# Decoder layer on one core: 22 instead of 20 of 24 gate tiles in pairs of seven products, with the products' banks, the t4 product and the next block's roots moved

## The chip, the cores and the metric

The kernel runs on one core of a Trainium2 chip. Its engines are PE (TensorE: matmuls, and PEld, the weight loads of the same engine), DVE (VectorE), ACT (ScalarE), POOL (GpSimd) and SP (SyncE, which issues nearly all DMAs here). The metric is the device time of one execution, in microseconds (us); lower is better.

## The reference

One layer of a hybrid decoder, for 2048 prompt tokens and 8 sequences of 8 sample tokens, in float32. With `xn = rmsnorm(x)`, one projection of 1024 inputs gives the columns of three branches and of 24 gate tiles; the branches (attention over a window of 128, a short convolution, a gated MLP with 128x128 position mixing) are merged through sigmoid gates:

```
r = rsqrt(mean(x*x) + EPS);  xn = x * r * norm_w
h = xn @ w_in                                   # q k v z_a | B C h z_b | u v_c z_c | g (3*1024 columns)
y_a, y_b, y_c = attention, conv, spatial MLP
a, b, c = (silu(z_i) * y_i) @ w_out_i           # 512 -> 1024 each
m = sigmoid(g_a)*a + sigmoid(g_b)*b + sigmoid(g_c)*c
y = x + m @ w_o
```

## The kernel before

**Blocks.** The tokens are worked in four blocks (`SBS`), one after the other: three of 512 tokens, and a last one of 512 prompt and 64 sample tokens (n = 576, in chunks of 288). Activations stand as channels x tokens, in tiles of 128 channels. Every float32 operand is split into a high and a low part (`split`: a cast on ACT, `wh` or `xh`, then a subtraction on DVE, `wl` or `xl`), and every product is three matmuls (L231 to L233: wh*xh, wh*xl, wl*xh).

**Weights.** `order()` lists the units of weights. `take` gives the next one and has the two behind it split (L222 on ACT, L223 on DVE) into one of four `wh`/`wl` buffers, and some more loaded (L140 on SP) into one of three `raw` buffers.

**Gate phase.** In each block 24 gate tiles (three for each of eight output tiles) are multiplied (8 k-tiles each) and put through a sigmoid, and `merge` multiplies each by its branch's output product (4 k-tiles, L231 to L233 again, then L897 and L903 on DVE). The first `SINGLES` = 4 tiles are done singly (`single`), the other 20 in ten pairs (`pair`). A pair treats two tiles, two halves of k and two halves of the tokens as a 2x2 block product in seven products of 4 k-tiles at half the tokens (`product`, L929 to L931) instead of eight. Four of the seven use sums of blocks: sums of weights, made on POOL (`halves`: s1 at L154, a difference in place at L155, s2 at L160, s2 again at L164), and sums of activations t1 to t4, made on DVE from `xh + xl` (`x_sums`: L840, L848 to L852 for t1 to t3 in `first`; L840 and L864 for t4 in `last`). Each t is split like any operand. The results are added up on DVE (L949 to L959), two sigmoids follow, and two merges.

**PSUM banks.** The seven products are put, in their order, on S0, pv, S1, S0, S1, pv, S0. A bank is free for the next product when the addition that reads it is done. Merges and single tiles use the three banks of `ps_mm`, transposes and the spatial products the two of `ps_tp`.

**Next block's roots.** `xrstd` gives pieces for the next block's `rsqrt`: four pieces (five ahead of the last block) that load 128 tokens into a `raw` buffer (L260 on SP) and sum their squares (L261 on ACT), then `fin` (L218 and L219 on POOL: scale and power) and `spread` (L275: transposes on PE that spread the roots over the partitions, and a copy on ACT).

**Order.** PE and SP run in the order in which the code is written; `later(delay, piece)` puts a piece behind so many ticks of written matmul work (a single tile is 1.5 ticks, a pair 2.75), and `flush` puts all pending ones at once. What DVE, ACT and POOL do is ordered by a scheduler when the kernel is built, and each engine then works its list strictly in that order. At the start of the gate phase there are still pieces pending from the MLP: the spatial products (L783, L784 on PE, two for each 128 tokens), their sums (L786, L787, L762 on DVE, in a tile `sp`) and the split into `br2`. The tiles `sp`, `s1` and `s2` share two buffers (tag `side`); t4 takes the buffer that the MLP's `suc` leaves when the last L762 has read it.

## Time and profile before

| | |
|---|---|
| runs | 2015.57 us median of 3 (2015.36 to 2016.91) |
| the profiled execution | 2013.36 us, its span 2011.6 us |
| PE | 1972.3 us busy, 98% of the span, 11771 matmuls |
| DVE, ACT, POOL | 68%, 47%, 17% busy |
| chain of work that ended last | PE 89%, DVE 5%, ACT 4% |
| gate phase until the first pair, block 0 | 253.88 to 290.98 us of the span |
| the same, block 2 | 1201.47 to 1249.57 us |

Start times are microseconds from the start of the span. A row of the timeline has the start, the duration, the engine, line and operation, out<-in, sizes, and in brackets how long the engine had been idle ahead of it and what released it. Matmuls overlap, so that the distance between two starts is their price, not the duration that stands in a row. In the table by windows the columns are the stretch, its length, the busy time and number of instructions of PE, PEld, DVE, ACT and POOL, the granted clock of TensorE (1.00 is full speed), the DMA share and GB/s. In the table of waits they are the waiting engine and line, what was waited for, and the total, the number and the longest in us.

### The profile page before, as it was taken

Reading aid. Unit: us, or ns where it says so; the run is one execution under the profiler, and the core shown is the slowest. Engines: PE = TensorE matmul, PEld = TensorE weight load, DVE = VectorE, ACT = ScalarE, POOL = GpSimd, SP = SyncE. Lnnn points to the kernel's source line nnn. Section 1 sums busy time; section 2 is a strip of 40 time slices with the busy share of each in tenths; the row PEclk is TensorE's granted clock in tenths of the full one; section 3 lists DMA queues with packets and bytes.
Section 4 is the critical chain, followed back from the end, with each engine's and each line's share of the span. In section 5 each row is a group of like instructions: output and inputs, shape, how many; then the busy total and the mean of one; then the engine's idle time right before and its main releaser. Section 6 shows DMA issues by size and latency. Waiting matters only on the chain.

```text
span 2011.6 us, 30272 instructions
## 1 busy us (share of the span) xinstructions
PE 1972.3 (98%) x11771; PEld 1765.4 (88%) x11771; DVE 1365.2 (68%) x2367; ACT 945.1 (47%) x1679; POOL 335.0 (17%) x294
## 2 busy tenths in 40 slices
PE   6999999999999999999999998999999999999999
PEld 5888889998888889998888887999889999999999
DVE  5688377875588558777478736777647873587772
ACT  4775254442576344444367524444347743333340
POOL 2100024320100004440200002442020000133310
PEclk9999999999999999999999998999999999999999
DMA  6222233336222232226322223223622242222233
GB/s 209 90 79 84 84 126 115 102 115 224 95 73 74 94 114 101 101 95 207 129 84 74 87 76 123 97 95 115 229 87 56 62 114 69 71 82 87 95 101 109
DMA packets 85711, 212.44 MB, mean 106 GB/s; under 512 B 18224, under 2 KB 23344, under 8 KB 85552
## 3 DMA queue, kind: packets, MB, share of 16 engines
q1 hardware_dynamic: 85536, 209.53, 32.4%
q8 instruction: 92, 1.51, 0.3%
q10 hardware_dynamic: 32, 0.98, 0.1%
q14 instruction: 51, 0.42, 0.1%
HBM read 201.46 MB, written 10.00 MB: 105 GB/s over the span
## 4 chain that ended last, share of the span: by engine, by line
PE 89%; DVE 5%; ACT 4%; DMA 1%; issue 1%; POOL 1%; SPq 0%; ACTq 0%; DVEq 0%; POOLq 0%
PE ps_mm L231 18%; PE ps_mm L232 18%; PE ps_mm L233 18%; PE pairS L929 4%; PE pairS L930 4%; PE pairS L931 4%; DVE wl L223 3%; PE pairpv L930 2%; PE pairpv L929 2%; PE pairpv L931 2%; PE ps_mm L353 2%; PE ps_mm L352 2%; PE ps_mm L351 2%; ACT wh L222 2%; PE wideS L353 1%; PE wideS L352 1%
## 5 line engine op out<-in xcount | busy, mean ns | idle before, releaser
L223 DVE TENSOR_TENSOR wl<-raw,wh 128x1024 fp32r<-128x1024 f32 (+1 forms) x416 | 461.7, 1118 | 272.1 <-ACT wh L222 269.1
L222 ACT CAST wh<-raw 128x1024 fp32r<-128x1024 f32 (+1 forms) x416 | 354.7, 866 | 539.1 <-PE ps_mm L232 232.7
L231 PE MATMUL ps_mm<-xh,wh 128*128 128x512 f32 (+1 forms) x1280 | 460.2, 360 | 0.0
L233 PE MATMUL ps_mm<-xh,wl 128*128 128x512 f32 (+1 forms) x1280 | 451.7, 353 | 0.0
L232 PE MATMUL ps_mm<-xl,wh 128*128 128x512 f32 (+1 forms) x1280 | 451.6, 353 | 0.0
L233 PEld LDWEIGHTS ps_mm<-xh,wl 128*128 128x128 f32 x1280 | 241.0, 188 | 30.7
L232 PEld LDWEIGHTS ps_mm<-xl,wh 128*128 128x128 f32 x1280 | 241.5, 189 | 27.1
L231 PEld LDWEIGHTS ps_mm<-xh,wh 128*128 128x128 f32 x1280 | 241.3, 189 | 27.3
L222 ACT CAST wh<-s 128x512 fp32r<-128x512 f32 x120 | 70.9, 621 | 194.1 <-PE ps_mm L232 116.5
L929 PE MATMUL pairS<-xh,wh 128*128 128x256 f32 (+1 forms) x480 | 140.1, 292 | 8.1 <-DVE ca L949 7.9
L218 POOL TENSOR_SCALAR vr<-vssq 128x1 f32<-128x1 f32 (+1 forms) x17 | 5.4, 316 | 804.9 <-ACT vn L795 804.5
L931 PE MATMUL pairS<-xh,wl 128*128 128x256 f32 (+1 forms) x480 | 137.2, 286 | 0.0
L930 PE MATMUL pairS<-xl,wh 128*128 128x256 f32 (+1 forms) x480 | 137.1, 286 | 0.0
L231 PE MATMUL ps_mm<-mhi,wh 128*128 128x512 f32 (+1 forms) x320 | 112.5, 352 | 0.9 <-ACT mhi L222 0.9
L233 PE MATMUL ps_mm<-mhi,wl 128*128 128x512 f32 (+1 forms) x320 | 112.5, 352 | 0.0
L897 DVE TENSOR_TENSOR t<-ps_mm,t 128x512 f32<-128x512 f32 (+1 forms) x120 | 70.8, 593 | 58.5 <-PE ps_mm L233 57.3
L929 PEld LDWEIGHTS pairS<-xh,wh 128*128 128x128 f32 x480 | 91.2, 190 | 14.5 <-DVE ca L949 13.2
L154 POOL TENSOR_TENSOR s<-raw 128x512 f32<-128x512 f32 x40 | 56.8, 1419 | 243.1 <-DMA raw<-in_wt 192.2
L164 POOL TENSOR_TENSOR s<-raw,s 128x512 f32<-128x512 f32 x40 | 67.6, 1690 | 160.2 <-DVE wl L223 160.2
L930 PEld LDWEIGHTS pairS<-xl,wh 128*128 128x128 f32 x480 | 91.4, 190 | 1.2
L929 PE MATMUL pairS<-xsum,wh 128*128 128x256 f32 (+1 forms) x320 | 91.7, 287 | 0.0
L930 PE MATMUL pairS<-xsum,wh 128*128 128x256 f32 (+1 forms) x320 | 91.6, 286 | 0.0
(280 smaller groups left out, 4638.7 us busy)
## 6 DMA issues: line engine op xcount, KB each, us to landing
raw<-in_wt SPq DMA_DIRECT2D x208, 512.0 KB
raw<-in_wout SPq DMA_DIRECT2D x96, 256.0 KB
raw<-in_wn SPq DMA_DIRECT2D x40, 512.0 KB
raw<-in_wo SPq DMA_DIRECT2D x32, 512.0 KB
xraw<-in_xn SPq DMA_DIRECT2D x12, 512.0 KB
xt<-in_xt SPq DMA_DIRECT2D x24, 256.0 KB
out_yt<-xt SPq DMA_DIRECT2D x24, 256.0 KB
xbuf<-in_xt SPq DMA_DIRECT2D x16, 256.0 KB
```

The lines of the kernel that those rows point to most:

```text
L164: add(combos["s2"], r0[:, H:], combos["s2"], ALU.subtract)
L222: nc.scalar.copy(hi, src)
L223: nc.vector.tensor_tensor(lo, src, hi.bitcast(F32), ALU.subtract)
L231: nc.tensor.matmul(o, wh[:, ws], rh(k, c0, c1), start=k == 0, stop=False)
L232: nc.tensor.matmul(o, wh[:, ws], rl(k, c0, c1), start=False, stop=False)
L233: nc.tensor.matmul(o, wl[:, ws], rh(k, c0, c1), start=False, stop=k == kts - 1)
L352: nc.tensor.matmul(o, xh[:, k, ts], wl, start=False, stop=False)
L353: nc.tensor.matmul(o, xl[:, k, ts], wh, start=False, stop=k == KT - 1)
L897: nc.vector.tensor_tensor(t[:, c0:c1], pa[:, : c1 - c0], t[:, c0:c1], ALU.mult)
L929: nc.tensor.matmul(o, wh[:, ws], rh(k), start=k == 0, stop=False)
L930: nc.tensor.matmul(o, wh[:, ws], rl(k), start=False, stop=False)
L931: nc.tensor.matmul(o, wl[:, ws], rh(k), start=False, stop=k == 3)
```

## The change

`SINGLES` goes from 4 to 2: the tiles 2 and 3 of each block become a pair, eleven pairs in place of ten. What `single(2)` used to do between its gate and its merge is now done by `sums_done`, after both singles with their merges: all pending pieces are put at once, and the two pieces of t4 follow at 0 and 0.5 ticks. The pieces `fin` and `spread` of the next block's roots are taken from the list of 0.75-tick steps and put 2 and 6 ticks behind `sums_done`. Within a pair, the t1 product goes to a bank of `ps_mm`; the product of 21 goes from S1 to S0, that of 22 from S0 to S1 and from the seventh place to the sixth; the t4 product comes last, and the sigmoid of the first tile is written ahead of it.

```diff
-SINGLES = 4
+SINGLES = 2
@@ gate_phase
-            for j, p in enumerate(xpieces):
+            for j, p in enumerate(xpieces[:-2]):
                 later(0.5 + 0.75 * j, p)
+            st["roots"] = xpieces[-2:]
...
+        def sums_done():
+            flush()
+            st["m"] = res.tile([P, KT, TMAX], F32, tag="mh", name="m")
+            for q in range(2):
+                later(0.5 * q, lambda q=q: last_sums(q))
+
+            for q, p in enumerate(st.get("roots", [])):
+                later(2.0 + 4.0 * q, p)
...
-            if j == 2:
-                flush()
-                st["m"] = res.tile([P, KT, TMAX], F32, tag="mh", name="m")
-                for q in range(2):
-                    later(0.25 + 0.75 * q, lambda q=q: last_sums(q))
...
+        def bank_of(bank):
+            if bank == "mm":
+                return ps_mm()
+            return psum.tile([P, 512], F32, tag=bank, name="pair" + bank, bufs=1)
...
@@ pair
             w = take("pair", (28 + j, 1))
             add(u, product("S1", w, 0, "t2"), p1, ALU.add)
             add(u3, p3, u, ALU.add)
-            p5 = product("S0", w, 1, "t1")
+            p5 = product("mm", w, 1, "t1")
             add(u5, p5, u, ALU.add)
             add(tb[:, hi], p5, u3, ALU.add)
             w = take("pair", (28 + j, 2))
-            add(ta[:, lo], product("S1", w, 0, "21"), p1, ALU.add)
+            add(ta[:, lo], product("S0", w, 0, "21"), p1, ALU.add)
+            w3 = take("pair", (28 + j, 3))
+            add(ta[:, hi], product("S1", w3, 0, "22"), u5, ALU.add)
+            nc.scalar.activation(ta, ta, AF.Sigmoid, bias=bias(j))
             add(tb[:, lo], product("pv", w, 1, "t4"), u3, ALU.add)
             nc.scalar.activation(tb, tb, AF.Sigmoid, bias=bias(j + 1))
-            w = take("pair", (28 + j, 3))
-            add(ta[:, hi], product("S0", w, 0, "22"), u5, ALU.add)
-            nc.scalar.activation(ta, ta, AF.Sigmoid, bias=bias(j))
...
         for j in range(SINGLES):
             single(j)
+        sums_done()
         for j in range(SINGLES, 24, 2):
             pair(j)
```

The scheduler's lists move with it. ACT in block 0, around the squares of the next block's tokens (`xraw`), before. The rows are from the first square on; `br2h` is the cast of a spatial result:

```order
L261 ACTIVATE xraw_2275,xr_2254<-xraw_2275 128x1024
L222 CAST wh_2391<-raw_2259 128x512
L222 CAST br2h_2251<-sp_2202 128x4x128
L261 ACTIVATE xraw_2311,xr_2254<-xraw_2311 128x1024
L222 CAST wh_2423<-raw_2295 128x1024
L222 CAST br2h_2251<-sp_2218 128x4x128
```

and in the changed kernel:

```order
L261 ACTIVATE xraw_2275,xr_2252<-xraw_2275 128x1024
L222 CAST wh_2319<-raw_2259 128x512
L222 CAST wh_2392<-s1_2321 128x512
L261 ACTIVATE xraw_2309,xr_2252<-xraw_2309 128x1024
L222 CAST br2h_2249<-sp_2200 128x4x128
L924 ACTIVATE t_2328<-ps_mm_2329,c_bg_159 128x512
```

The second square now stands ahead of the cast of the first spatial result, and the casts of the first pair's weights ahead of both.

DVE in block 0, the end of the list ahead of the first pair's additions, before (the sums for t4 are `xq` and `xsum4`; the first addition is L949):

```order
L864 TENSOR_TENSOR xq_2533<-xq_2533,xsum_2056 128x512
L223 TENSOR_TENSOR wl_2553<-s1_2512,wh_2552 128x512
L223 TENSOR_TENSOR xsum4_2495<-xq_2533,xsum4_2495 128x512
L223 TENSOR_TENSOR wl_2582<-raw_2427,wh_2581 128x512
L223 TENSOR_TENSOR wl_2582<-raw_2429,wh_2581 128x512
L897 TENSOR_TENSOR t_2519<-ps_mm_2563,t_2519 128x512
L223 TENSOR_TENSOR wl_2615<-s2_2554,wh_2614 128x512
L223 TENSOR_TENSOR wl_2654<-raw_2560,wh_2653 128x1024
L949 TENSOR_TENSOR ca_2579<-pairS1_2623,ca_2579 128x256
L950 TENSOR_TENSOR cb_2580<-pairpv_2601,ca_2579 128x256
```

and in the changed kernel, from the first use of s2 to the addition that frees pv (L959 and L960 are the old L949 and L950):

```order
L223 TENSOR_TENSOR wl_2393<-s2_2394,wh_2392 128x512
L787 TENSOR_TENSOR sp_2248<-ps_tp_2431,sp_2248 128x256
L787 TENSOR_TENSOR sp_2248<-ps_tp_2438,sp_2248 128x256
L223 TENSOR_TENSOR wl_2454<-raw_2257,wh_2453 128x512
L762 TENSOR_TENSOR sp_2248<-sp_2248,suc_1798 128x512
L223 TENSOR_TENSOR wl_2454<-raw_2259,wh_2453 128x512
L864 TENSOR_TENSOR xq_2493<-xq_2493,xsum_2056 128x512
L223 TENSOR_TENSOR br2l_2250<-sp_2248,br2h_2249 128x4x128
L223 TENSOR_TENSOR xsum4_2466<-xq_2467,xsum4_2466 128x512
L864 TENSOR_TENSOR xq_2493<-xq_2493,xsum_2056 128x512
L223 TENSOR_TENSOR wl_2500<-s2_2394,wh_2499 128x512
L959 TENSOR_TENSOR ca_2451<-pairS1_2508,ca_2451 128x256
```

The last spatial sums, the weights of parts 2 and 3 and the sums for t4 now stand between the first pair's second part and its first addition; before, the spatial work ended twenty rows earlier.

POOL in block 2 before, from `fin` for the four full pieces (`xr`) on, with the first pair's sums of weights:

```order
L218 TENSOR_SCALAR xr_11008<-xr_11008 128x4
L219 TENSOR_TENSOR xr_11008<-xr_11008,mhalf_78 128x4
L154 TENSOR_TENSOR s1_11274<-raw_11183 128x512
L155 TENSOR_TENSOR raw_11183<-raw_11181,raw_11183 128x512
L160 TENSOR_TENSOR s2_11316<-s1_11274,raw_11181 128x512
L218 TENSOR_SCALAR xr_11008<-xr_11008 64x1
L219 TENSOR_TENSOR xr_11008<-xr_11008,mhalf_78 64x1
L164 TENSOR_TENSOR s2_11316<-raw_11181,s2_11316 128x512
```

and in the changed kernel:

```order
L160 TENSOR_TENSOR s2_11280<-s1_11207,raw_11143 128x512
L164 TENSOR_TENSOR s2_11280<-raw_11143,s2_11280 128x512
L218 TENSOR_SCALAR xr_11138<-xr_11138 128x4
L219 TENSOR_TENSOR xr_11138<-xr_11138,mhalf_78 128x4
L218 TENSOR_SCALAR xr_11138<-xr_11138 64x1
L219 TENSOR_TENSOR xr_11138<-xr_11138,mhalf_78 64x1
L154 TENSOR_TENSOR s1_11447<-raw_11395 128x512
```

`fin` moved from ahead of the first pair's sums of weights, and from between them, to behind them and ahead of the second pair's.

## Prediction

> **What bounds the kernel now.** I read the page first, then the waits, then the timeline at the two places where PE stands longest in the gate phase.

> ```profile
> span 2011.6 us, 30272 instructions
> PE 1972.3 (98%) x11771; PEld 1765.4 (88%) x11771; DVE 1365.2 (68%) x2367; ACT 945.1 (47%) x1679; POOL 335.0 (17%) x294
> PEld pairS L929 <- DVE ca L949: 13.2, 25, 1.6
> PE pairS L929 <- DVE ca L949: 7.9, 18, 1.3
> PE ps_tp L275 <- POOL xr L219: 7.7, 1, 7.7
> ```

> PE is busy 98% of the span, so the time falls only by fewer or cheaper matmuls or by stops of PE that go. Two stops concern this change. Product 21 waits 25 times, its weight loads 13.2 us in all, for the addition L949 that frees S1. And once PE stands 7.7 us for the roots. That is in block 2:

> ```profile
> 1224.84 0.98 SPq L260 DMA_DIRECT2D xraw<-in_xn  x1
> 1232.63 1.05 ACT L261 ACTIVATE xraw<-xraw 64x1024 f32<-64x1024 f32 x1
> 1235.50 0.36 PE L275 MATMUL ps_tp<-c_ident,xr 64*128 64x64 f32 x1 [7.67 <-POOL xr L219]
> 1228.10:1231.50 3.40, 0.00 (x0) 0.00 (x0) 1.50 (x3) 1.25 (x3) 1.98 (x2) 1.00 0.08 29
> 1231.50:1241.70 10.20, 6.20 (x15) 4.83 (x16) 4.66 (x7) 3.15 (x7) 3.30 (x4) 0.50 0.16 51
> ```

> The fifth load of tokens is issued at 1224.84, squared at 1232.63, and the transpose goes at 1235.50. After an empty stretch the clock is 0.50 for 10.2 us, in which PE works 6.20 us: half of that, 3.1 us, is lost too.

> **Gains, term by term.** *A: fewer columns.*

> ```profile
> 282.82 0.39 PE L231 MATMUL ps_mm<-xh,wh 128*128 128x512 f32 x1
> 290.98 0.28 PE L929 MATMUL pairS<-xh,wh 128*128 128x256 f32 x1
> 307.17 0.28 PE L929 MATMUL pairS<-xh,wh 128*128 128x256 f32 x1
> 317.24 0.40 PE L231 MATMUL ps_mm<-br0h,wh 128*128 128x512 f32 x1
> 322.71 0.28 PE L929 MATMUL pairS<-xh,wh 128*128 128x256 f32 x1
> 1766.61 0.29 PE L231 MATMUL ps_mm<-xh,wh 128*128 128x288 f32 x1
> 1776.15 0.29 PE L929 MATMUL pairS<-xh,wh 128*128 128x288 f32 x1
> 1847.97 0.29 PE L929 MATMUL pairS<-xh,wh 128*128 128x288 f32 x1
> 1865.49 0.29 PE L929 MATMUL pairS<-xh,wh 128*128 128x288 f32 x1
> ```

> A single with its merge lasts 290.98 - 282.82 = 8.16 us, an unhindered pair 322.71 - 307.17 = 15.54: one more pair saves 0.78 us in blocks 0 to 2. In block 3 a single is 9.54 and a pair 17.52: 1.56. Sum 2.3 + 1.6 = 3.9 us.

> *B: L949 no longer in the way.* A product lasts a seventh of 317.24 - 307.17, 1.44 us. 21 now goes to S0, whose reader is the copy of product 11, four products earlier. 22 on S1 needs the addition that 21 needed, but starts 1.44 us later; against the longest wait of 1.6 us that leaves 0.2. So the 13.2 us go (7.9 by the PE row of the same wait, my lower end). The t1 product's bank was last used by the pair before, a whole pair ago: no cost.

> *C: roots.* `fin` is put 2 and `spread` 6 ticks behind the singles, so that PE comes to it in the third pair, over 30 us after the first began, while the last load and square take 8 (1224.84 to 1232.63): 7.7 + 3.1 = 10.8 us.

> Gains: 27.9 us.

> **Losses.** *D: the first pair of blocks 0 to 2.* The two singles that go were also the time in which DVE worked off the MLP's spatial sums and made t4. That work stays, and PE arrives 16.8 us earlier. Block 0:

> ```profile
> 253.88 0.39 PE L231 MATMUL ps_mm<-xh,wh 128*128 128x512 f32 x1
> 273.19 0.39 PE L231 MATMUL ps_mm<-xh,wh 128*128 128x512 f32 x1
> 263.45 0.33 SPq L260 DMA_DIRECT2D xraw<-in_xn  x1
> 269.12 2.99 SPq L260 DMA_DIRECT2D xraw<-in_xn  x2
> 272.83 1.06 ACT L261 ACTIVATE xraw<-xraw 128x1024 f32<-128x1024 f32 x1 [1.22 <-DMA xraw<-in_xn]
> 267.95 1.06 ACT L261 ACTIVATE xraw<-xraw 128x1024 f32<-128x1024 f32 x1 [1.11 <-DMA xraw<-in_xn]
> 265.49 0.69 DVE L762 TENSOR_TENSOR sp<-sp,suc 128x512 f32<-128x512 f32 x1
> 270.53 1.23 DVE L223 TENSOR_TENSOR wl<-raw,wh 128x1024 fp32r<-128x1024 f32 x1
> 271.68 0.68 DVE L223 TENSOR_TENSOR br2l<-sp,br2h 128x512 fp32r<-128x512 f32 x1
> 280.04 0.69 DVE L840 TENSOR_TENSOR xq<-xh,xl 128x512 f32<-128x512 f32 x1
> 280.64 0.69 DVE L223 TENSOR_TENSOR wl<-raw,wh 128x512 fp32r<-128x512 f32 x1
> 284.39 1.30 POOL L160 TENSOR_TENSOR s<-s,raw 128x512 f32<-128x512 f32 x1
> 291.74 1.62 DVE L223 TENSOR_TENSOR xsum<-xq,xsum 128x512 fp32r<-128x512 f32 x1
> 296.82 0.41 DVE L949 TENSOR_TENSOR ca<-pairS,ca 128x256 f32<-128x256 f32 x1
> 297.94 0.41 DVE L953 TENSOR_TENSOR t<-pairS,cb 128x256 f32<-128x256 f32 x1
> ```

> The two singles end at 273.19; two more spatial groups of 0.48 and the first pair could start at 274.15, 16.8 us ahead of 290.98, its seventh product at 274.15 + 6 * 1.44 = 282.8. What DVE has by then: in its new list 36 instructions stand from the first spatial split (`br2l`) to the addition that frees pv for t4: 21 of 512 elements, 14 of 256, one of 1024. From start to start one of 512 takes 0.60 (280.04 to 280.64), three of 256 take 1.12, so 0.37 each, and one of 1024 takes 1.15: 12.6 + 5.2 + 1.2 = 19.0 us. The list can begin when ACT has cast the first spatial result. Before, that went ahead of the second square; now it stands behind it. That square started at 267.95, waiting for tokens issued at 263.45. The third came 3.7 us after its issue (269.12 to 272.83) with no weights loaded just ahead, as now holds for the second: 267.15. A square (1.05) and the cast (0.6) later DVE starts, near 268.75, where its inputs (265.49 + 0.6) would let it start at 266.1.

> 268.75 + 19.0 = 287.75. To that come waits inside the list: `sp` of the last tokens now takes the buffer of s1, so DVE waits for L160, and L160 for the `sp` before it: 1.3 less one instruction of 0.6 that lies beside it, 0.8 with the handing over. Two casts behind weight casts on ACT: 0.6. And while POOL works DVE is slower (1.62 where 0.60 is usual, at 291.74): one such loss for L160 and for L164, about 0.6 each. So t4 starts near 290.4 instead of 282.8: 7.6 us. By the same count `wl` of s2 ends near 281.3 and L959 near 288: PE stops at the spatial products, at t2, some 2.5 us at 22 (21 ends at 285.5) and 1 us at t4. Ends: with no wait in the list 287.75 - 282.8 = 4.9; with a full loss of 1.0 at four POOL instructions 10. I take 7.6, since the waits follow from the lists. Three blocks: 22.8 (14.7 to 30).

> *E: block 3.* No squares, so the list starts 2.6 us earlier by the same rows; six products last 9.6 (17.52 less two merges, each a third of a single of 9.54, leaves 11.2; a seventh is 1.6) instead of 8.6. That leaves 7.6 - 2.6 - 1.0 = 4.0 (1 to 7).

> *F: the second pair.*

> ```profile
> 294.02 0.89 SPq L140 DMA_DIRECT2D raw<-in_wt  x2
> 300.38 1.30 POOL L154 TENSOR_TENSOR s<-raw 128x512 f32<-128x512 f32 x1 [7.57 <-DMA raw<-in_wt]
> ```

> On SP the fourth load of tokens (in block 2 the fifth too) now waits for a `raw` buffer of the first pair, and the second pair's weights stand behind it; on POOL `fin` stands ahead of that pair's sums. The second `raw` buffer comes free with the split behind L959, near 289.5; 6.4 us (294.02 to 300.38) bring the weights by 296, three sums of 1.3 s2 by 300. The second pair starts near 297.3 and needs s2 at its third product, 300.2: hidden, at nearly no distance. 0 (0 to 2). `spread` is far behind all this.

> *G: half clock behind the stops of D.*

> ```profile
> 1528.50:1531.90 3.40, 1.85 (x11) 1.48 (x11) 2.32 (x7) 3.32 (x6) 0.00 (x0) 0.99 0.08 2
> 1531.90:1535.30 3.40, 3.40 (x17) 3.38 (x16) 1.85 (x3) 1.94 (x4) 0.00 (x0) 0.50 0.00 0
> 357.00:360.40 3.40, 2.77 (x24) 2.56 (x22) 3.40 (x5) 1.57 (x2) 0.77 (x1) 1.00 0.19 31
> ```

> A stretch of 3.4 us in which PE was busy 1.85 us was followed by 3.4 us at 0.50; one with 2.77 was not. The stops ahead of 22 and of t4, 2.5 and 1 us with one product between, leave PE about 1.5 us busy in 3.4: that can be enough. Half a stretch of PE work is at most 1.7 us, and part of it lies beside a wait for DVE. I take 1 us in each of three blocks: 3 (0 to 6).

> [...]

> **Sum.** Losses 22.8 + 4.0 + 3.0 = 29.8, less 27.9: 1.9 us more, call it 2. The profiled execution (2013.36 us) would become 2015; it is 2.2 us below the median of the runs, and I forecast on the median: 2015.57 + 2 = 2017.6. That is 0.1%, and 0.2% or 4 us is about what a measurement of this kernel can tell from no change. Only the sign of a small difference of two sums near 30 us decides; either of them is much surer than the difference. The likeliest case has its own range: D from 6 to 9.5 per block and G from 0 to 6 give 2010 to 2026.

> **Rivals.** *1, faster: DVE catches up.* Place: DVE's list from 268.75. If tokens land earlier, the squares are out of the way and the list loses nothing inside: D is 4.9 per block, E 2, G 0. 27.9 - 16.7 = 11 us gained, 2004.4; half way, 2008. It decides from (27.9 - 4.0) / 3 = 8.0 us for D and G of one block; I have 8.6. For it: the work alone ends 2.7 us sooner than I put it. Against: each list is strict, and the square of 267.95 did wait for its DMA.

> *2, slower: the clock.* The stops of a first pair (near 1, 1, 2, 3 and 1 us within 20) put several stretches below half busy, as at 1231.50, where 0.50 held for 10.2 us. PE then loses some 3 us in each of three blocks in place of 1: plus 6 to 9, 2025. Against: while PE waits for DVE a slow clock costs nothing. [...]

> *3, slower: B doesn't come.* If L959 ends more than one product later than L949 did, 22 takes over the waits of 21: B 0, plus 13.2, 2031. Against it: waits of 1.6 at most against 1.44.

> **Chances.** Forecast 0.48 (of it no change 0.33, slower 0.15), rival 1 0.28 (faster 0.25, no change 0.03), rival 2 0.18, rival 3 0.06. Faster by over 0.2%: 0.25; within: 0.36; slower: 0.39. The range takes in rival 1 half way and rival 2: 2006 to 2028.

> **What the profile after would show.** A: pairs 15.54 us apart. B: no wait of a product for L959 or S1 outside the first pairs. C: no wait of L275, no 0.50 near 1231. D: PE stops of 6 to 9 us in the first pair of blocks 0 to 2, before t2, 22 and t4, with DVE busy throughout. E: about half of that in block 3. F: second pairs without stops. G: a stretch of 0.50 behind the first pairs. I am wrong if the first pairs run within 3 us of 10.07, if they last over 21 us, or if second pairs stop too.

## The result, and the profile after

The changed kernel takes 2021.68 us, median of 12 runs (2018.44 to 2024.33), against 2017.24 us for the kernel before in the same comparison: ratio 1.0023, 95% interval 1.0015 to 1.0032. It is slower by 0.23%, 4.4 us. The profiled execution took 2023.21 us; 1.05 us of its distance to the one before was there already when PE began its second group of matmuls, before anything that was changed.

The page's head, and from the waits of PE the rows that concern the gate phase (engine, line, what was waited for; total, number, longest in us):

```profile
span 2021.5 us, 30607 instructions
PE 1969.0 (97%) x11867; PEld 1768.0 (87%) x11867; DVE 1388.9 (69%) x2411; ACT 953.1 (47%) x1697; POOL 357.0 (18%) x310
...
PE ps_tp L783 <- DVE sp L787: 11.0, 7, 3.0
PE pairS L939 <- DVE ca L959: 5.9, 4, 2.2
PE pairS L939 <- ACT wh L222: 4.2, 4, 1.3
PE ps_mm L231 <- DVE t L898: 1.6, 1, 1.6
```

PE works 3.3 us less than before and yet the span is 9.9 us longer. The wait of L275 is gone, and of the waits for the addition L949 (now L959) four are left on PE, three of them in first pairs and one in block 2's second. New are seven stops, 11.0 us in all, at the spatial products (L783), and stops inside the first pairs.

What the gains look like, in the timeline of PE (two neighbouring pairs of block 0) and in two stretches of block 2, the same as shown of before:

```profile
332.13 0.28 PE L939 MATMUL pairS<-xh,wh 128*128 128x256 f32 x1
347.67 0.28 PE L939 MATMUL pairS<-xh,wh 128*128 128x256 f32 x1
...
1228.10:1231.50 3.40, 1.48 (x8) 1.34 (x9) 3.30 (x8) 1.18 (x2) 0.00 (x0) 1.00 0.45 154
1231.50:1241.70 10.20, 8.13 (x56) 7.06 (x55) 8.80 (x18) 3.73 (x8) 2.72 (x2) 1.00 0.15 51
```

Pairs stand 15.54 us apart, as an unhindered pair did before, and the clock near 1231 is 1.00 where it was 0.50.

What the losses look like: block 0 ahead of and in the first pair, one sequence put together from ACT, DVE, PE and POOL.

```profile
269.10 1.06 ACT L261 ACTIVATE xraw<-xraw 128x1024 f32<-128x1024 f32 x1 [2.42 <-DMA xraw<-in_xn]
270.16 0.60 ACT L222 CAST br2h<-sp 128x512 fp32r<-128x512 f32 x1
270.80 0.69 DVE L223 TENSOR_TENSOR br2l<-sp,br2h 128x512 fp32r<-128x512 f32 x1 [1.79 <-ACT br2h L222]
271.59 0.76 DVE L786 TENSOR_TENSOR sp<-ps_tp,c_bsb 128x256 f32<-128x256 f32 x2
272.26 0.75 DVE L787 TENSOR_TENSOR sp<-ps_tp,sp 128x256 f32<-128x256 f32 x2
272.83 0.35 PE L783 MATMUL ps_tp<-wsp,vbuf 128*128 128x256 f32 x1 [2.15 <-DVE sp L787]
...
280.36 0.69 DVE L223 TENSOR_TENSOR br2l<-sp,br2h 128x512 fp32r<-128x512 f32 x1
281.13 1.66 POOL L160 TENSOR_TENSOR s<-s,raw 128x512 f32<-128x512 f32 x1 [20.82 <-DVE br2l L223]
282.82 0.62 ACT L222 CAST wh<-s 128x512 fp32r<-128x512 f32 x1 [1.67 <-POOL s L160]
283.49 0.39 PE L939 MATMUL pairS<-xsum,wh 128*128 128x256 f32 x1 [1.32 <-ACT wh L222]
...
290.23 0.41 DVE L959 TENSOR_TENSOR ca<-pairS,ca 128x256 f32<-128x256 f32 x1
290.79 0.55 PE L939 MATMUL pairS<-xh,wh 128*128 128x256 f32 x1 [2.23 <-ACT xraw L261]
```

Three stops follow each other. The square of late tokens holds the cast `br2h`, that holds the split `br2l`, and only then comes the sum that frees the bank for the next spatial product. Later POOL waits 20.8 us for a buffer that the third `br2l` frees, and t2's product waits for the weights that POOL makes in it. At last 22 waits for bank S1, which L959 frees at 290.64 (its row names an ACT instruction that ended about then; in blocks 1 to 3 the same stop is put down to L959). Counted as distances between starts beyond the usual ones, the stops are 2.3 us at the spatial products and 1.5 + 0.4 + 2.4 in the first pair, and with two stretches of 0.50 block 0 loses 9.9 us. Blocks 1 and 2 lose 8.2 us each there without a slow stretch.

### The profile page after: what moved, and what is told of

Same layout as the page of the kernel before. It is cut to its first block, busy times and chain, and to the rows that moved or that the text cites. A ratio compares the mean times of both kernels' runs of the same rounds, so it can differ in the third digit from the quotient of the medians.

```text
span 2021.5 us, 30607 instructions
## 1 busy us (share of the span) xinstructions
PE 1969.0 (97%) x11867; PEld 1768.0 (87%) x11867; DVE 1388.9 (69%) x2411; ACT 953.1 (47%) x1697; POOL 357.0 (18%) x310
## 4 chain that ended last, share of the span: by engine, by line
PE 88%; DVE 4%; ACT 3%; DMA 2%; issue 1%; POOL 1%; SPq 0%; DVEq 0%; ACTq 0%; POOLq 0%
PE ps_mm L231 17%; PE ps_mm L232 17%; PE ps_mm L233 17%; PE pairS L939 4%; PE pairS L941 4%; PE pairS L940 4%; PE pairpv L941 2%; PE pairpv L939 2%; PE pairpv L940 2%; PE ps_mm L353 2%; PE ps_mm L352 2%; PE ps_mm L351 2%; PE wideS L353 1%; PE wideS L351 1%; PE wideS L352 1%; DVE wl L223 1%
## 5 line engine op out<-in xcount | busy, mean ns | idle before, releaser
L223 DVE TENSOR_TENSOR wl<-raw,wh 128x1024 fp32r<-128x1024 f32 (+1 forms) x420 | 478.1, 1147 | 258.9 <-ACT wh L222 255.4
L231 PE MATMUL ps_mm<-xh,wh 128*128 128x512 f32 (+1 forms) x1200 | 431.5, 360 | 0.0
L233 PE MATMUL ps_mm<-xh,wl 128*128 128x512 f32 (+1 forms) x1200 | 423.2, 353 | 0.0
L232 PE MATMUL ps_mm<-xl,wh 128*128 128x512 f32 (+1 forms) x1200 | 423.0, 353 | 0.0
L233 PEld LDWEIGHTS ps_mm<-xh,wl 128*128 128x128 f32 x1200 | 225.7, 188 | 28.9
L232 PEld LDWEIGHTS ps_mm<-xl,wh 128*128 128x128 f32 x1200 | 226.3, 189 | 25.3
L231 PEld LDWEIGHTS ps_mm<-xh,wh 128*128 128x128 f32 x1200 | 225.9, 188 | 25.5
L940 PE MATMUL pairS<-xl,wh 128*128 128x256 f32 (+1 forms) x528 | 151.4, 287 | 0.0
L231 PE MATMUL ps_mm<-mhi,wh 128*128 128x512 f32 (+1 forms) x320 | 112.5, 352 | 0.9 <-ACT mhi L222 0.9
L223 DVE TENSOR_TENSOR wl<-s,wh 128x512 fp32r<-128x512 f32 x132 | 93.2, 728 | 12.8 <-ACT wh L222 10.8
L941 PEld LDWEIGHTS pairS<-xh,wl 128*128 128x128 f32 x528 | 101.2, 192 | 0.0
L154 POOL TENSOR_TENSOR s<-raw 128x512 f32<-128x512 f32 x44 | 61.4, 1396 | 225.2 <-DMA raw<-in_wt 162.2
L164 POOL TENSOR_TENSOR s<-raw,s 128x512 f32<-128x512 f32 x44 | 72.1, 1638 | 136.9 <-DVE wl L223 136.9
```

Of the source, the lines that this page charges most:

```text
L154: add(s1, r1[:, :H], r1[:, H:], ALU.add)
L164: add(combos["s2"], r0[:, H:], combos["s2"], ALU.subtract)
L223: nc.vector.tensor_tensor(lo, src, hi.bitcast(F32), ALU.subtract)
L231: nc.tensor.matmul(o, wh[:, ws], rh(k, c0, c1), start=k == 0, stop=False)
L232: nc.tensor.matmul(o, wh[:, ws], rl(k, c0, c1), start=False, stop=False)
L233: nc.tensor.matmul(o, wl[:, ws], rh(k, c0, c1), start=False, stop=k == kts - 1)
```

## The experiments

Ratios are to the kernel before, run on the same chip between them, with 95% intervals; what one kernel is worth against another, in us, is worked out from these ratios, since the medians of before lie between 2014 and 2017 us in the comparisons. Beside them I use the time of each block in the profiled execution, from the first `wide` product of one block to that of the next (the last block: to the last matmul), worked out from the starts of PE's instructions. Slow stretches (granted clock 0.50) fell in different places in the profiled executions and, by an estimate from the 0.50, move a block by up to half their length (1.7 us for 3.41). One of 3.41 us, begun between 1511 and 1537, is in block 3 of six rows (before, after, e10, e1, e9, e8) and not in the others.

| | 0 | 1 | 2 | 3 |
|---|---|---|---|---|
| before | 471.98 | 473.30 | 490.13 | 536.80 |
| after | 477.00 | 477.65 | 484.46 | 541.91 |
| banks alone (e2) | 468.28 | 470.30 | 485.39 | 531.67 |
| roots alone (e3) | 474.74 | 473.75 | 478.88 | 535.98 |
| banks and roots (e10) | 468.41 | 470.68 | 475.81 | 533.25 |
| four singles, rest as changed (e1) | 469.84 | 472.14 | 477.47 | 533.22 |
| no t4 (e4) | 476.95 | 477.43 | 483.16 | 537.78 |
| own `sp` (e5) | 478.85 | 481.05 | 484.94 | 540.44 |
| both (e9) | 472.50 | 473.86 | 478.32 | 535.90 |
| early squares (e6) | 473.26 | 474.64 | 479.25 | 540.27 |
| early spatial products (e7) | 471.90 | 474.38 | 479.88 | 535.09 |
| all three (e8) | 470.60 | 474.02 | 478.08 | 536.63 |

**The gains, part by part.** Banks alone: the kernel before with the part of the diff inside `pair` and `bank_of`.

> The kernel before with the new banks and the new order of the products in a pair alone (t1 on a bank of ps_mm, 21 on S0, 22 on S1 as the sixth, t4 last); four singles and roots as before. My theory: the waits of product 21 for L949 go, 12.7 to 13.8 us less, about 2004 us, ratio 0.9935; every pair's products take 10.07 us (11.15 in the last block). Rival: 22 takes over the wait, ratio 0.998 to 1.000.

Measured 0.9925 (0.9913 to 0.9937), 15.1 us less. In the waits of PE no product of a pair is left; the root stall is:

```profile
PE ps_tp L275 <- POOL xr L219: 7.6, 1, 7.6
```

Roots alone:

```diff
-            for j, p in enumerate(xpieces):
+            for j, p in enumerate(xpieces[:-2]):
...
+        for q, p in enumerate(st.get("roots", [])):
+            later(2.0 + 4.0 * q, p)
         for j in range(SINGLES, 24, 2):
```

> The kernel before with fin and spread of the next block's roots put 2 and 6 ticks behind the four singles, nothing else. My theory: the stall of 7.7 us in block 2 and the stretch of 0.50 behind it go, 10.8 us less, about 2006.5 us, ratio 0.9946. Rival a: the stop comes back in the pairs and the clock falls there, 0 to 3 us less. Rival b: only the wait itself counts, 7.7 us less, ratio 0.996.

Measured 0.9954 (0.9942 to 0.9966), 9.3 us less; block 2 takes 11.25 us less, the others change by 2.8 at most, of both signs. The wait for L275 is gone from the list, and product 21 waits as before:

```profile
PE pairS L930 <- DVE ca L950: 8.3, 19, 1.3
```

Both together:

> The kernel before with the new banks and order of products and with the later roots, and nothing else: four singles, t4 made where it was. If the two gains add (0.9925 and 0.9954 by themselves): 0.988 of the kernel before, about 1990 us; by the times between the blocks' starts in those two runs 27 us less, 0.9865. It would be some 2 to 4 us under the kernel with four singles and earlier t4 pieces, whose profile still shows 0.4 to 0.9 us stops at the spatial products and at the split br2l in each block. If later roots bring stops of their own once the pairs run unhindered: 0.990 to 0.992.

Measured 1991.13 us, 0.9881 (0.9868 to 0.9894). The gains add: 15.1 + 9.3 = 24.4 us by themselves, 24.0 together (0.0119 of 2014.45). What is left of waits inside pairs is one row:

```profile
PE pairS L935 <- DVE ca L955: 0.3, 1, 0.3
```

**The pairing undone**, all else as changed:

```diff
-SINGLES = 2
+SINGLES = 4
...
         for j in range(SINGLES):
             single(j)
-        sums_done()
+            if j == 1:
+                sums_done()
```

> The changed kernel with four singles again: banks, order of products, later roots and the place of t4's pieces (behind two singles) stay as changed, only the pairing of tiles 2 and 3 is undone. My theory: the product stops (13.8 us over 40 pairs) and the root stall with its half clock (10.8) stay gone, and the first pairs, which now start 16 us after the spatial sums begin to fall due, run without stops: 24.6 us under the kernel before, about 1992.6 us, ratio 0.988 (0.986 to 0.990). Rival (the losses of 38 us in the changed kernel come from the new banks or the moved roots, not from the pairing): the first pairs stop here too, 2005 to 2020 us.

Measured 1992.85 us, 0.9893 (0.9880 to 0.9905). The first pairs run without stops (15.54 us each in blocks 0 to 2), so the losses belong to the pairing: 1.0023 against 0.9893 is 26 us, spread over all four blocks (7.2, 5.5, 7.0 and 8.7 in the table). It is a little behind banks and roots alone by the table (1.4, 1.5, 1.7 and 0.0 us; the intervals of the two ratios overlap), since pending pieces and t4, put two singles earlier, now wait at the merge of the third single:

```profile
PE ps_mm L232 <- DVE br2l L223: 2.0, 3, 0.7
PE ps_tp L783 <- DVE sp L787: 0.9, 3, 0.4
```

**Is it the length of DVE's list?** That was step D. t4's sums are left out:

```diff
-            for q in range(2):
-                later(0.5 * q, lambda q=q: last_sums(q))
+            sums["t4"] = sums["t2"]
```

> The changed kernel without the sums of activations t4: the product t4 takes t2's tiles instead (same matmuls), so that ten instructions of DVE's list between the spatial sums and the first pair's additions (two xq, four L864, two splits, 0.6 us each, 4.8 us) and two casts on ACT are left out. My theory (the first pair waits because DVE's list is longer than the time that PE gives it): the stop ahead of t2 and the one of 2.4 us ahead of 22 go, 5 us less in each of blocks 0 to 2, 2 to 4 in block 3, 2 in the second pair of block 2: 17 to 23 us under the changed kernel, about 2002 us, 0.992 to 0.994 of the kernel before. The stop at the spatial products (2.2 us per block) stays, since it lies ahead of t4's work. Rival (the tile buffers shared with sp, or late tokens, hold the list, not its length): within 6 us of the changed kernel, 0.999 to 1.002 of the kernel before.

Measured 2016.65 us, 1.0008 (0.9999 to 1.0017): 3 us under the changed kernel by the ratios, 5 by the medians, not 17 to 23. The rival's range was met. Block 0, first DVE at the first pair, then POOL and PE at the second:

```profile
275.96 0.69 DVE L223 TENSOR_TENSOR br2l<-sp,br2h 128x512 fp32r<-128x512 f32 x1 [1.79 <-ACT br2h L222]
282.82 0.76 DVE L786 TENSOR_TENSOR sp<-ps_tp,c_bsb 128x256 f32<-128x256 f32 x2 [1.40 <-POOL s L160]
288.43 0.41 DVE L958 TENSOR_TENSOR ca<-pairS,ca 128x256 f32<-128x256 f32 x1
...
295.23 1.29 POOL L154 TENSOR_TENSOR s<-raw 128x512 f32<-128x512 f32 x1 [2.73 <-DMA raw<-in_wt]
300.19 0.39 PE L940 MATMUL pairpv<-vst,wl 128*128 128x256 f32 x1 [0.97 <-DVE wl L223]
```

Of 4.8 us of work taken out (eight instructions of DVE, not ten), 2.0 reach the addition that frees S1, counted from the gate phase's first product (35.31 us to 33.36); the rest turned into idle time behind the cast and the shared buffer. PE's starts show what became of it (us, blocks 0 / 1 / 2 / 3; a pair counts from its start to the next pair's):

| | gate phase until the first pair | first pair | second pair |
|---|---|---|---|
| unhindered | 20.3 (blocks 0 to 2) | 15.5, block 3 17.5 | 15.5, block 3 17.5 |
| after | 24.2 / 23.5 / 23.5 / 29.8 | 21.5 / 20.5 / 20.5 / 22.0 | 15.5 / 15.5 / 17.6 / 17.5 |
| no t4 (e4) | 24.4 / 23.7 / 24.3 / 27.8 | 17.9 / 17.7 / 17.9 / 20.3 | 17.9 / 17.4 / 17.9 / 17.5 |
| own `sp` (e5) | 23.3 / 23.3 / 23.1 / 27.0 | 24.3 / 23.9 / 23.4 / 24.9 | 15.5 / 15.5 / 15.5 / 17.5 |
| both (e9) | 23.3 / 24.1 / 23.2 / 27.0 | 17.8 / 15.6 / 16.8 / 17.6 | 15.5 / 15.5 / 15.5 / 17.5 |

So the first pairs did become 2.6 to 3.6 us shorter in blocks 0 to 2, and the second pairs of blocks 0 and 1 gave 2.3 and 1.9 of it back. Their weights are loaded when they were before (the first load is issued at 287.33, in the changed kernel at 287.32, and L154 starts at 295.23, there at 294.71), and the pair that comes 3.2 us earlier waits for them.

**Is it the shared buffer?**

```diff
-                t = side("sp", [P, 4, P])
+                t = tmp("sp", [P, 4, P])
```

> The changed kernel with the tile sp of the spatial sums taken from the five buffers of tag tmp instead of the two of tag side, which s1 and s2 then have alone. New theory (a chain through the shared buffers: cast br2h, split br2l, then the buffer is free for s2 in L160, then s2's cast and split, which t2 and behind it 22 wait for): the stops ahead of t2 (1.7 to 1.9 us) and of 22 (2.4) in blocks 0 to 2 mostly go, 3.5 to 4.5 us each, 1 to 2 in block 3; the spatial stop stays; 12 to 15 us under the changed kernel, about 0.995 of the kernel before. First theory (DVE's list is too long): the work only changes places, t4 waits instead; 0 to 4 us under the changed kernel, 1.000 to 1.002.

Measured 2024.97 us, 1.0055 (1.0043 to 1.0068): no gain, by the ratios 6 us worse than the changed kernel (3 by the medians). POOL makes s2 at once, t2's stop is gone, and yet the addition that frees S1 starts about where it did (0.7 and 0.9 us later in blocks 0 and 1, 0.7 earlier in block 2, counted from the gate phase's first product):

```profile
259.55 1.29 POOL L160 TENSOR_TENSOR s<-s,raw 128x512 f32<-128x512 f32 x1
287.07 1.75 DVE L223 TENSOR_TENSOR wl<-s,wh 128x512 fp32r<-128x512 f32 x1
288.75 1.74 DVE L864 TENSOR_TENSOR xq<-xq,xsum 128x512 f32<-128x512 f32 x1
290.42 0.41 DVE L959 TENSOR_TENSOR ca<-pairS,ca 128x256 f32<-128x256 f32 x1
PE pairS L939 <- DVE ca L959: 15.6, 4, 5.8
291.20:294.60 3.40, 3.40 (x16) 3.15 (x16) 3.40 (x7) 0.89 (x2) 0.42 (x1) 0.50 0.23 55
```

PE comes to 22 earlier and waits there in one stop instead of two, 15.6 us in all. Part of what the list gained went to slower DVE: two of its last instructions take 1.75 and 1.74 us while POOL already works on the second pair's sums (286.99 to 289.94); in the changed kernel, where POOL starts these sums at 294.71, after L959, the same two take 0.68 each (289.62 and 289.02). And the longer stop brings slow stretches with it, 6.83 us at 0.50 in every block. At half their length, an estimate, that is at most 13.7 us against 5.1 for the changed kernel's three new ones, enough for the whole difference between the two. Neither theory was right alone.

**Both at once**, the two diffs above together.

> The changed kernel with both single edits: sp from tag tmp, and the t4 product on t2's tiles, t4's sums left out. What the two showed apart: 5 us less and 3 us more. Theory of two bounds (the chain through the shared buffers and the length of DVE's list end within 2 us of each other, so that either alone hides the other): together they take away the stops inside the first pairs, 4 to 5 us per block, and the half clock behind them; the spatial stop of 2.2 us stays: 12 to 20 us under the changed kernel, 0.993 to 0.997 of the kernel before. Theory that they simply add: 0 to 4 us under it, 1.000 to 1.003. Theory that late tokens hold all of it: no change, 1.002.

Measured 2000.76 us, 0.9927 (0.9915 to 0.9939): by the ratios 19 us under the changed kernel, where the two by themselves gave 3 less and 6 more. The clock explains a part of this gap, not most of it: with every slow stretch inside the blocks counted at half its length (an estimate), the table gives about 3 us less than the changed kernel for each edit alone and 17 for both. The two bounds, the chain through the shared buffers and the length of the list, end within about 2 us of each other, and each hid what was taken from the other. The addition that frees S1 now comes 3.2 to 3.8 us earlier in blocks 0 to 2 (first row, of block 0), and the second pairs run unhindered: the first of their weight loads is issued at 275.81 in place of 287.32, so what had held s2 had held the `raw` buffers too. Of the waits of PE in the first pairs and ahead of them this is left:

```profile
285.64 0.42 DVE L958 TENSOR_TENSOR ca<-pairS,ca 128x256 f32<-128x256 f32 x1
PE pairS L938 <- DVE ca L958: 3.0, 2, 2.0
PE ps_tp L783 <- DVE sp L787: 9.2, 7, 2.0
```

**The squares.** Loads and squares of the next tokens go among the MLP's first products:

```diff
@@ chunk_phase
+        if sb + 1 < len(SBS):
+            st, xpieces = xrstd(sb + 1)
+            roots.update(st, roots=xpieces[-2:])
+            for j, p in enumerate(xpieces[:-2]):
+                later(0.5 + 1.5 * j, p)
@@ gate_phase
-            st, xpieces = xrstd(sb + 1)
-            for j, p in enumerate(xpieces[:-2]):
-                later(0.5 + 0.75 * j, p)
-            st["roots"] = xpieces[-2:]
+            st = roots
```

> The changed kernel with the token loads and squares of the next block put among the MLP's first products, ahead of the gate phase (fin and spread stay 2 and 6 ticks behind the singles). New theory (late tokens hold ACT, ACT holds the cast of the spatial sums, and so the chain): the spatial stop falls from 2.2 to about 1 us, the chain ends 1 to 1.5 us earlier, the half clock of block 0 goes, the second pair of block 2 runs without stops (2.4); block 3 as it is: 8 to 12 us under the changed kernel, 0.996 to 0.998 of the kernel before. Rival (squares don't matter, since ACT has room): within 3 us of the changed kernel, 1.001 to 1.003.

Measured 2010.92 us, 0.9978 (0.9968 to 0.9988), 9 us less than the changed kernel. The cast is hardly held (0.69 us of idle DVE in place of 1.79) and the spatial stops shrink from 11.0 us to 4.6, 3.1 of them in block 3, which has no squares; block 2's second pair runs without stops:

```profile
270.18 0.69 DVE L223 TENSOR_TENSOR br2l<-sp,br2h 128x512 fp32r<-128x512 f32 x1 [0.69 <-ACT br2h L222]
PE ps_tp L788 <- DVE sp L792: 4.6, 6, 3.1
```

**The spatial products one tick earlier** (`AT_SPATIAL` is 1.0 in place of 2.0), and **all three edits**, own `sp`, early squares and this:

> The changed kernel with AT_SPATIAL at 1.0 in place of 2.0: every spatial product is written one tick (5.4 us of PE) earlier, among the first single's products. New theory: br2l, L160 and s2 come up to 5 us earlier, the first pairs run without stops but for the list's length; some short stops of 0.5 to 1 us at the first spatial products, whose input vbuf is split at 255.4 to 261.5: 15 to 25 us under the changed kernel, 0.990 to 0.995 of the kernel before. Rival (the spatial products now wait for vbuf, as much as they waited before): within 5 us, 1.000 to 1.002.

> The three edits before together: sp from tag tmp, squares ahead of the gate phase, spatial products one tick earlier. New theory: no stop over 0.5 us is left in the first and second pairs of blocks 0 to 2, and of 38 us of losses 30 to 36 go: 1987 to 1993 us, 0.986 to 0.989 of the kernel before, up to 4 us under the kernel with four singles. If something that none of them touches holds the first pairs (DVE's list by its length), 5 us per block stay: 2003 to 2008, 0.994 to 0.997.

Measured 0.9956 (0.9942 to 0.9969) and 0.9929 (0.9916 to 0.9941). One tick earlier gives 13 us, a little short of the 15 to 25 forecast: it takes the stop ahead of 22 nearly away, while s2 still waits for the buffer (first row, of e7). With all three, 19 us of the loss go, not 30 to 36: the spatial products come so early that they wait in turn (second row, of e8), 5.1 us in all, so that the first pairs of blocks 0 to 2 still start 2.1 us late, and they still take 17.0 to 17.8 us. The waits in the profile do not account for all that is left.

```profile
276.75 1.64 POOL L160 TENSOR_TENSOR s<-s,raw 128x512 f32<-128x512 f32 x1 [8.03 <-DVE br2l L223]
...
263.41 0.36 PE L788 MATMUL ps_tp<-wsp,vbuf 128*128 128x256 f32 x1 [1.52 <-DVE sp L792]
```

The fastest version measured is the kernel before with banks and roots alone, 0.9881 of it (four singles with the rest as changed, 0.9893, can't be told from it); no version with 22 tiles in pairs came nearer than 0.9929 with t4's sums and 0.9927 without them.

## Why the prediction was right, and where it was not

The forecast was 2 us slower with 4 us as the bound of what can be told; 4.4 us came. The direction was right and most of the terms, but a sign that rests on a small difference of two sums near 30 us is in part luck: the gains came out within 1 us, the losses were some 2.5 us (medians) to 7 us (profiles) larger than forecast. Against banks and roots alone, what the pairing costs net per block is 8.59, 6.97, 8.65 and 8.66 us (table); with the saved columns (0.78, in block 3 1.56) added back, 9.4, 7.8, 9.4 and 10.2.

- **A** held: pairs 15.54 us apart, 17.51 in block 3.
- **B** held: 13.2 forecast, 15.1 measured alone (12.7 to 17.5 by the interval). The lower end of 7.9, read from the PE row of the same wait, was too low; the PEld row was the better guide. Rival 3 appeared only in the first pairs and once, 0.85 us, in block 2's second.
- **C** held: 10.8 forecast, 9.3 measured (6.9 to 11.7 by the interval), 11.25 in block 2's own time.
- **D with G**: 8.6 per block forecast, 9.4, 7.8 and, without F, 7.4 measured. D alone forecast t4 36.5 us behind the gate phase's first product (290.4 - 253.88), 7.6 late; it came at 38.6, 37.1 and 37.0, in block 0 behind two slow stretches. The first pair starts 3.2 to 3.9 us late, at the spatial products, which the step names and its signs leave out; its products take 16.0, 15.1 and 15.1 us, 5 to 6 beyond the usual 10.07. For the sum it doesn't matter where on the way PE stands, since it counts to the list's end. The list itself was read rightly, 36 instructions, with 2.9 to 3.4 us of waits in it where I had 1.4; DVE was not "busy throughout". So the size is right, the cause half right: I had read one bound, the list's length. There was a second of nearly the same length: through the two `side` buffers each `sp` waits for the `br2l` of an earlier one. A forecast that counts one of two equal bounds comes out right; what one then expects of removing that bound does not come, as the run without t4 shows.
- **E** failed: 4.0 forecast (1 to 7), 10.2 measured. The step took the list of blocks 0 to 2 and started it 2.6 us earlier, as there are no squares. Block 3's list starts only 1.6 us earlier (its first `br2l` 14.25 us behind the gate phase's first product, not 15.8), and it is another list: its sample tokens bring a fifth spatial result, so that 40 instructions stand up to the addition that frees pv, and many are wider. They keep DVE busy 22.5 us in place of 19.6, with 4.3 us of waits among them. In block 3, too, the buffers and DVE's order hold the sums:

```profile
1758.03 0.69 DVE L223 TENSOR_TENSOR br2l<-sp,br2h 128x512 fp32r<-128x512 f32 x1
1759.31 0.75 DVE L786 TENSOR_TENSOR sp<-ps_tp,c_bsb 128x256 f32<-128x256 f32 x2
1760.54 0.36 PE L783 MATMUL ps_tp<-wsp,vbuf 128*128 128x256 f32 x1 [3.04 <-DVE sp L787]
1787.84 0.40 PE L231 MATMUL ps_mm<-br0h,wh 128*128 128x288 f32 x1 [1.58 <-DVE t L898]
```

  A spatial stop of 3.0 us, a slow stretch behind it, 2.6 us in the pair and a merge that waits make up the 10 us. By the table no t4 takes 4.1 us of block 3 away, own `sp` 1.5, both 6.0. Which of the two weighs more there is not shown: the changed kernel has two slow stretches in block 3, no t4 none, and own `sp` one of 6.83 us.
- **F** failed in block 2 alone: 0 (0 to 2) forecast, 2.0 measured, at two products of the second pair. The weights behind the fifth load of tokens came late, and POOL's sums with them:

```profile
1253.76 1.28 POOL L154 TENSOR_TENSOR s<-raw 128x512 f32<-128x512 f32 x1 [2.93 <-DMA raw<-in_wt]
1258.71 0.39 PE L941 MATMUL pairpv<-vst,wl 128*128 128x256 f32 x1 [0.65 <-DVE wl L223]
1265.34 0.39 PE L939 MATMUL pairS<-xh,wh 128*128 128x256 f32 x1 [0.85 <-DVE ca L959]
```

  With the squares out of the gate phase these stops are gone. A second pair that stops was one of the signs of being wrong that the prediction named.
- **G**: three new slow stretches of 3.41 us, two in block 0 and one in block 3, not one in each of blocks 0 to 2. Half of a stretch is 1.7 us, so by this estimate they cost 5 at most, inside the range; the places are not those forecast. Rival 2, 6 to 9 us more from the clock, did not come.

By the profiles, then: gains 28 (A 3.9, B and C 24.1 by the table), losses 36.8 (9.4 + 7.8 + 9.4 + 10.2), 8.8 us net, and 1.05 at the start of this execution make the 9.9 us between the two spans. Medians say 4.4; the profiled execution of before lies 3.9 us under its median, that of after 1.5 over its own. E is the term that was mis-sized, by 6 us, and F by 2. Rival 1, DVE catching up, did not come: even 4.8 us of work taken from its list brought the addition that frees S1 only 1.2 to 2.0 us forward in blocks 0 to 2.

## What to carry to other kernels

Before work is pulled together, count what the removed filler hid on every strict list and in every shared buffer, since two bounds of nearly equal length hide each other: undo each alone and both together before naming a cause. Look one pair further as well, since time won in the first pair can be lost to weights that land no earlier, and compare the slow stretches before a few microseconds are read as a cause. A buffer class with two entries, shared by a producer that runs ahead and a chain that runs late, turns into an order between them that no line of the code states. And take a change apart: two of its parts were worth 24 us, and the third gave them back.

## What the runs showed of the hardware

```profile
270.13:273.54 3.41, 1.26 (x8) 0.87 (x7) 2.64 (x7) 1.27 (x4) 0.00 (x0) 1.00 0.43 154
273.54:276.95 3.41, 3.41 (x11) 2.84 (x11) 3.14 (x7) 1.67 (x3) 0.00 (x0) 0.50 0.16 58
1533.05:1536.46 3.41, 1.86 (x10) 1.31 (x10) 2.50 (x8) 3.33 (x6) 0.00 (x0) 1.00 0.12 4
1536.46:1539.87 3.41, 3.41 (x17) 3.40 (x16) 1.60 (x2) 2.10 (x4) 0.00 (x0) 0.50 0.01 2
765.06:768.47 3.41, 1.96 (x17) 1.75 (x15) 3.41 (x7) 1.87 (x4) 0.00 (x0) 1.00 0.75 225
768.47:771.88 3.41, 2.23 (x17) 2.09 (x18) 3.41 (x8) 2.00 (x4) 2.37 (x2) 1.00 0.64 222
1785.65:1789.06 3.41, 1.83 (x14) 1.60 (x13) 3.41 (x8) 2.31 (x4) 1.67 (x1) 1.00 0.00 0
1789.06:1792.48 3.42, 3.42 (x28) 3.42 (x28) 2.64 (x6) 1.02 (x2) 0.00 (x0) 1.00 0.61 170
```

Stretches with PE busy 1.20, 1.26, 1.37 and 1.86 us of 3.41 are followed by 0.50. Those with 1.96 to 2.12 are not, but neither is the one at 1785.65, with 1.83. The kernel before shows the same distance: its clock falls to 0.50 at 1231.48, for 10.24 us, and at 1531.86, for 3.41 us, the two 300.37 us or 88 times 3.413 apart, behind stretches of 3.41 us with PE busy 0.00 and 1.87; behind one with 2.10, at 357.67, it stayed at 1.00. From 40 us to the last product these are all the falls in the two profiles, and apart from the one at 1785.65 every stretch at full clock with PE busy below 1.96 us was followed by 0.50. So PE's busy time, in which the ends of matmuls are modelled, gives no sharp border: 1.83 us was not followed by 0.50, 1.86 and 1.87 were. The stop ahead of 22 left PE busy 1.37 us in one stretch of block 0, at 287.19, and 0.50 followed; in block 1 the same stop lay across a border of the grid, at 768.47, with PE busy 1.96 and 2.23 us on its two sides, and the clock stayed at 1.00. So what a stop cost here depended on where it fell. The four stretches ahead of the changed kernel's slow ones were 1.20 to 1.86 us busy, none idle throughout.
